# Key and receptance weights: the low halves written by an adding transfer instead of a subtraction on VectorE

## Chip, cores and metric

One core of a Trainium2 chip runs the kernel; the seven others are idle. The metric is the device time of one execution in microseconds (us), taken several times; for the profiled execution there is also a trace, with a span from the first to the last instruction.

## What is computed

The reference is a decoder trunk of two layers over 512 tokens with 1024 channels, in float32: a layer with RWKV-7 time mixing and one with causal differential attention, each between two half-step SwiGLU blocks. The change concerns the time mixing alone, cut here to what matters:

```python
dx = h_prev - h
r, k, v = einsum('sbtc,scd->sbtd', h[None] + dx[None] * mu[:3, None, None, :], w_rkv)   # three 1024x1024 products
...
kk = normalised(k * k_k);  k = k * (1 + (a - 1) * k_a)
y = wkv7_scan(r, decay, k, v, -kk, kk * a)     # S_t = S diag(w) + (S a) b^T + v k^T ; y = S r, 16 heads of 64
...
return (y * g) @ w_o
```

The scan is not done token by token. It is cut into 8 chunks of 64 tokens, and inside a chunk the recurrence becomes small matrix products and the inverse of a triangular matrix per head and chunk.

## The kernel before

**Products in three passes.** TensorE gets a float32 product as three passes over numbers in a reduced format (fp32r): `mm3` (L214 to L217) multiplies high weight by high input, high weight by low input, low weight by high input. So every weight block is kept as two tiles: `whi`, the weight rounded to the reduced format, and `wlo`, what is left of it.

**How a weight block gets there.** `wblock` (L144) has SP load 256 columns of a weight (1 MB) from HBM into a `wraw` buffer (two of them). `halves` (L153) makes, for each of the two 128-column blocks, `whi` with a copy on ACT (L161) and `wlo` with a subtraction on DVE (L162). There are three `whi` and three `wlo` buffers; a block's buffers come free when PE has done its 24 matmuls.

**The time mixing, in order** (`rwkv`). The value product comes first, then the key product (the call of `proj` after `xk = mixed(1)`; eight blocks, here k0 to k7), then receptance (after `xr = mixed(0)`; r0 to r7). In each, one pair of blocks is done row by row, its two blocks taking turns (`by_rows`: k6 with k7, r0 with r1). When a key block is done, `key_done` works on it (`key_cb`) and on the scores of the block two before it (`scores`), which end in DRAM as `md_d`, `am_d` and `boxes`. When a receptance block p is done, `r_done` multiplies it into `Rb` on DVE (L884; the tile is `sR`, called "p's multiply" below).

**The inverses.** `invert` (L829) inverts 128 triangular 32x32 matrices at once on DVE in 31 steps of a multiply (L841) and an add (L842), then copies the transposed result (L844) and stores it into `boxes` with 8 DMAs issued by POOL (L849). It runs twice: `inv0` for heads 0 to 7 (temporary tile `nr_t`), `inv1` for heads 8 to 15 (temporary `nr_a`). Its steps are handed out between the other work (`run`).

**The units.** `wkv` does 16 units (chunk, half of the heads), in stages. Unit 0 begins with a matmul (L971) on `bx`, which SP loads from `boxes` (L946), so after inv0. Units on the second half of the heads come from the fifth unit on. `norm` (L1042 to L1049) has POOL multiply BK with `sR` (L1044, waits for the multiplies of p = 0 to 3 or 4 to 7).

**What sets the order.** A scheduler puts each engine's instructions in a row when the kernel is built; at run time each engine goes through its row and waits by semaphores. DMAs are issued by an engine's queue in that same row: SP's go through a hardware queue (q1), POOL's through a software queue (q0). Before the change the boxes DMAs are the only ones on q0.

```python
self.nc.scalar.copy(hi[:, ks], raw[:, :, c : c + P])                                  # L161, ACT
(eng or self.nc.vector).tensor_sub(lo[:, ks], raw[:, :, c : c + P], hi[:, ks].bitcast(F32))   # L162, DVE
```

Of the kernel before, what the change touches and what calls it, by code (L numbers as in the profile page):

```python
# [10 lines left out]
F32 = mybir.dt.float32  # L11
F32R = mybir.dt.float32r
AF = mybir.ActivationFunctionType
ALU = mybir.AluOpType
PSUM = bass.MemoryType.PSUM

P = 128
T = 512
C = 1024
# [6 lines left out]
class Net:  # L26
# [116 lines left out]
    def wblock(self, src, kt, cols, eng=None, raws=None):  # L143


        raws = raws or [self.tl(self.wp, "wraw", (P, 8, 256), bufs=2)[:, :kt]]
        n = kt // len(raws)
        src = src.rearrange("(k p) f -> p k f", p=P)
        for i, raw in enumerate(raws):
            self.nc.sync.dma_start(raw[:, :, :cols], src[:, i * n : i * n + n, :])  # L150
        return self.halves(raws, kt, cols, eng)

    def halves(self, raws, kt, cols, eng=None):  # L153
        n = kt // len(raws)
        out = []
        for c in range(0, cols, P):
            hi = self.tl(self.wp, "whi", (P, 8, P), F32R, bufs=3)
            lo = self.tl(self.wp, "wlo", (P, 8, P), F32R, bufs=3)
            for i, raw in enumerate(raws):
                ks = slice(i * n, i * n + n)  # L160
                self.nc.scalar.copy(hi[:, ks], raw[:, :, c : c + P])  # L161
                (eng or self.nc.vector).tensor_sub(lo[:, ks], raw[:, :, c : c + P], hi[:, ks].bitcast(F32))  # L162
            out.append((hi, lo))
        return out

# [397 lines left out]
    def rwkv(self, xs, prm):  # L563
# [6 lines left out]
        with ExitStack() as outer:  # L570
# [17 lines left out]
            kt = pa.enter_context(tc.tile_pool(name="kt", bufs=1))  # L588
# [23 lines left out]
            def halves(src):  # L612
                m = src.shape[0]
                hi = self.tl(self.gp, "xgh", dt=F32R, bufs=XB)[:m]
                lo = self.tl(self.gp, "xgl", dt=F32R, bufs=XB)[:m]
                nc.scalar.copy(hi, src)
                nc.vector.tensor_sub(lo, src, hi.bitcast(F32))
                return hi, lo
# [7 lines left out]
            raw = self.tl(self.wp, "wraw", (P, 8, 256), bufs=2)  # L626
# [7 lines left out]
            z = shifted(*pwa, P)  # L634
            nc.scalar.activation(z[0:64], z[0:64], AF.Tanh)
            zh, zl = halves(z)
            pgr = self.ps()
            for k in range(KT):
                self.mm3(pgr[0:64], lr[:, 0, k, :], lr[:, 1, k, :], xg[k][0], xg[k][1], k == 0, k == KT - 1)
            z = shifted(*pg0, P)  # L640
            nc.scalar.activation(z, z, AF.Sigmoid)
            gh, gl = halves(z)
            for k in range(KT):
                nc.sync.dma_start(d["x"][k], xs[k])
# [15 lines left out]
            def mixed(s, eng=None):  # L660

                out = []
                for k in range(KT):
                    i = s * KT + k
                    t = self.tl(kt, "xmt", bufs=2)
                    if s == 2:
                        nc.vector.tensor_scalar_mul(t, h[k][:, 1:], self.omu[:, i : i + 1])
                    else:
                        nc.scalar.activation(t, h[k][:, 1:], AF.Copy, scale=self.omu[:, i : i + 1])
                    nc.vector.scalar_tensor_tensor(t, h[k][:, 0:T], self.v("mu", i), t, ALU.mult, ALU.add)  # L670
                    out.append(self.split(self.gp, t, "xg", XB, eng))
                return out
# [6 lines left out]
            raw = self.tl(self.wp, "wraw", (P, 8, 256), bufs=2).rearrange("p k f -> p (k f)")[:96, :C]  # L679
# [7 lines left out]
            for p in range(KT + 3):  # L687
                if p < KT:
                    c = slice(p * P, (p + 1) * P)
# [7 lines left out]
                if p >= 3:  # L697
                    q = p - 3
                    c = slice(q * P, (q + 1) * P)
# [166 lines left out]
                    run(inv0, 1 if p == 5 else 8)  # L866

            xk = mixed(1)
            last = self.proj(prm["w_rkv"][1], xk, key_done, flush=False, by_rows=C - 256)
            xr = mixed(0)  # L870

            def feed(k):
# [11 lines left out]
                nc.vector.tensor_mul(Rb[:, p, :, 1:], Rb[:, p, :, 1:], ch(ps))  # L884
                run(inv1, 5)

            self.proj(prm["w_rkv"][0], xr, r_done, by_rows=0, feed=feed)
            pa.close()
            run(inv1, 40)
            zs, wb0 = self.wkv(A, BK, Rb, X, fac, d, prm["w_o"])  # L890
# [527 lines left out]
```

## Time and profile before

| | us |
|---|---|
| runs | 2167.19, 2161.10, 2167.46; median 2167.19 |
| profiled execution, device time | 2161.41 |
| its span | 2159.7 (1.7 lie outside) |
| busy in the span: PE | 2108.7 (98%) |
| DVE | 1196.4 (55%) |
| ACT | 821.9 (38%) |
| POOL | 221.4 (10%) |
| granted TensorE clock, mean | 0.991 of full |

PE is busy nearly all the time, so a change can only move the time where PE stands still or is slowed; the shares of the other engines are means over stages that differ. The stage of this change lies between about 440 and 640 us of the span: the key product up to 528, scores up to 537, receptance from 537 to 586, and then the units.

### The profile page before, as it was taken

The numbers are of one execution on the slowest core, as the hardware profiler recorded it, in microseconds if no ns is written. First come the engines' busy times: TensorE is split into PE (matmuls) and PEld (weight loads), VectorE is DVE, ScalarE is ACT, GpSimd is POOL, SyncE is SP. The second block draws the span as 40 slices with busy tenths as digits, with TensorE's granted clock in tenths as the row PEclk, the third lists the DMA queues.
The fourth block names the chain that finished last, engine by engine and source line by source line (L and its number), as shares of the span: only waits on it lengthen the run. The fifth ranks groups of instructions, "written<-read, shape, count | busy, mean of one in ns | idle before, by whom it ended". The sixth has DMA issues, their size and how long they took to land.

```text
span 2159.7 us, 26494 instructions
## 1 busy us (share of the span) xinstructions
PE 2108.7 (98%) x10479; PEld 1770.8 (82%) x10479; DVE 1196.4 (55%) x1876; ACT 821.9 (38%) x1395; POOL 221.4 (10%) x259
## 2 busy tenths in 40 slices
PE   9999999999879999999999999999999999999999
PEld 7888888777779888888888988888889778888887
DVE  6445555798947765444445535445346855444443
ACT  5222324588225444322224443223235854322222
POOL 1101000000332301100000001001010210100000
PEclk9999999999979999999999999999999999999999
DMA  7732333335587632222223223222322112323332
GB/s 251 237 98 88 117 103 103 121 123 136 120 201 187 179 124 89 95 95 96 97 93 103 93 87 98 96 97 97 97 92 85 40 50 91 97 96 97 98 98 78
DMA packets 268760, 239.83 MB, mean 111 GB/s; under 512 B 56922, under 2 KB 253692, under 8 KB 268636
## 3 DMA queue, kind: packets, MB, share of 16 engines
q1 hardware_dynamic: 267868, 236.05, 35.0%
q0 software_dynamic: 768, 2.10, 0.7%
q8 instruction: 82, 1.34, 0.3%
q14 instruction: 42, 0.34, 0.0%
HBM read 202.98 MB, written 28.84 MB: 107 GB/s over the span
## 4 chain that ended last, share of the span: by engine, by line
PE 87%; DVE 6%; ACT 3%; DMA 3%; issue 1%; POOL 1%; SPq 0%; DVEq 0%; ACTq 0%
PE ps L215 27%; PE ps L216 26%; PE ps L217 26%; ACT s L1209 1%; PE ps L1013 1%; DMA boxes<-x 1%; PE ps L977 0%; PE ps L989 0%; PE ps L1012 0%; PE ps L999 0%; POOL boxes L849 0%; DVE x L842 0%; PE ps L1003 0%; PE ps L971 0%; DMA wraw<-in_rwkv_w_rkv_dram 0%
## 5 line engine op out<-in xcount | busy, mean ns | idle before, releaser
L215 PE MATMUL ps<-xgh,whi 128*128 128x512 f32 x1688 | 658.5, 394 | 1.6 <-ACT whi L161 1.0
L216 PE MATMUL ps<-xgl,whi 128*128 128x512 f32 x1688 | 656.0, 390 | 0.0
L217 PE MATMUL ps<-xgh,wlo 128*128 128x512 f32 x1688 | 648.4, 390 | 0.0
L161 ACT CAST whi<-wraw 128x1024 fp32r<-128x1024 f32 (+2 forms) x296 | 303.4, 1029 | 874.2 <-PE ps L216 578.1
L162 DVE TENSOR_TENSOR wlo<-wraw,whi 128x1024 fp32r<-128x1024 f32 (+2 forms) x296 | 427.2, 1447 | 92.4 <-ACT whi L161 83.2
L215 PEld LDWEIGHTS ps<-xgh,whi 128*128 128x128 f32 x1688 | 316.5, 188 | 74.2 <-ACT whi L161 2.7
L216 PEld LDWEIGHTS ps<-xgl,whi 128*128 128x128 f32 x1688 | 317.0, 188 | 66.7 <-issue 1.7
L217 PEld LDWEIGHTS ps<-xgh,wlo 128*128 128x128 f32 x1688 | 316.8, 188 | 65.9
L414 POOL TENSOR_TENSOR u<-u,g 128x512 f32<-128x512 f32 x88 | 124.7, 1417 | 1370.2 <-ACT whi L161 996.3
L216 PE MATMUL ps<-actl,whi 128*128 128x512 f32 x656 | 255.2, 389 | 0.0
L215 PE MATMUL ps<-acth,whi 128*128 128x512 f32 x656 | 254.7, 389 | 0.0
L217 PE MATMUL ps<-acth,wlo 128*128 128x512 f32 x656 | 254.7, 389 | 0.0
L413 DVE TENSOR_TENSOR u<-ps,R 128x512 f32<-128x512 f32 x88 | 60.8, 691 | 287.3 <-PE ps L217 287.3
L456 DVE SCALAR_TENSOR_TENSOR x<-ps,x 128x512 f32<-128x512 f32 x88 | 60.5, 691 | 212.0 <-PE ps L217 212.0
L217 PEld LDWEIGHTS ps<-acth,wlo 128*128 128x128 f32 x656 | 123.1, 188 | 25.7
L215 PEld LDWEIGHTS ps<-acth,whi 128*128 128x128 f32 x656 | 123.1, 188 | 25.6
L216 PEld LDWEIGHTS ps<-actl,whi 128*128 128x128 f32 x656 | 123.1, 188 | 25.4
L215 PE MATMUL ps<-whi,xgh 128*128 128x256 f32 (+1 forms) x384 | 122.8, 323 | 0.2 <-DVE mx L1204 0.2
L216 PE MATMUL ps<-wlo,xgh 128*128 128x256 f32 (+1 forms) x384 | 122.4, 319 | 0.0
L217 PE MATMUL ps<-whi,xgl 128*128 128x256 f32 (+1 forms) x384 | 122.2, 318 | 0.0
L410 DVE TENSOR_TENSOR g<-ps,R 128x512 f32<-128x512 f32 x88 | 60.8, 691 | 109.8 <-PE ps L217 109.7
L222 ACT CAST acth<-u 128x512 fp32r<-128x512 f32 x88 | 54.9, 624 | 124.3 <-POOL u L414 124.2
(332 smaller groups left out, 2262.7 us busy)
## 6 DMA issues: line engine op xcount, KB each, us to landing
wraw<-in_ffn_w_in_dram SPq DMA_DIRECT2D x87, 1024.0 KB, 5.1
wraw<-in_ffn_w_out_dram SPq DMA_DIRECT2D x34, 1024.0 KB, 5.1
boxes<-nr_a SPq DMA_DIRECT2D x64, 192.0 KB, 3.5
wraw<-in_rwkv_w_rkv_dram SPq DMA_DIRECT2D x12, 1024.0 KB, 5.8
wraw<-in_ffn_w_out_dram SPq DMA_DIRECT2D x12, 768.0 KB, 4.4
wraw<-in_w_kv_dram SPq DMA_DIRECT2D x8, 1024.0 KB, 5.4
am_d<-nsq SPq DMA_DIRECT2D x16, 256.0 KB, 2.4
AM<-am_d SPq DMA_DIRECT2D x16, 256.0 KB, 4.4
```

The costliest lines, as they stand in the source:

```text
L161: self.nc.scalar.copy(hi[:, ks], raw[:, :, c : c + P])
L162: (eng or self.nc.vector).tensor_sub(lo[:, ks], raw[:, :, c : c + P], hi[:, ks].bitcast(F32))
L215: mm(ps, wh, xh, start=start, stop=False)
L216: mm(ps, wh, xl, start=False, stop=False)
L217: mm(ps, wl, xh, start=False, stop=stop)
L222: self.nc.scalar.copy(hi, src)
L410: nc.vector.tensor_mul(g, pg, self.R)
L413: nc.vector.tensor_mul(u, pu, self.R)
L414: nc.gpsimd.tensor_mul(u, u, g)
L456: nc.vector.scalar_tensor_tensor(x, ps, 0.5, x, ALU.mult, ALU.add)
L1013: mm(py[:, p, cols], V[:, p, :], KM[:, p, cols], start=c == 0, stop=True)
L1209: nc.scalar.activation(sc, sc, AF.Exp, scale=-1.0, bias=mx[h][:, i, m : m + 1], accum_out=sm[:, h, i, m : m + 1])
```

## The change

For the key and receptance weights, and for no others, `halves` gets `eng = "add"`. ACT writes `whi` as before, and then a second time the same block with its sign turned, rounded to the same format: the negative high half, into `wlo`. Then POOL issues a DMA that reads the block's 128 columns from HBM once more and adds it to what stands in `wlo` (128 x 8 x 128 numbers, 512 KB, in pieces of 512 bytes). That makes 16 subtractions on DVE fewer, 16 activations on ACT more, and 16 DMAs on POOL's queue more. In the changed kernel all lines from L153 on stand 5 lines lower in the time mixing (boxes DMAs L854, `norm` L1049 and L1054, multiplies L889, inverse L846 to L849), the turned copy is L164 and the adding DMA L165.

```diff
@@ wblock @@
-        return self.halves(raws, kt, cols, eng)
+        return self.halves(raws, kt, cols, eng, src)
@@ halves @@
                 self.nc.scalar.copy(hi[:, ks], raw[:, :, c : c + P])
-                (eng or self.nc.vector).tensor_sub(lo[:, ks], raw[:, :, c : c + P], hi[:, ks].bitcast(F32))
+                if eng == "add":
+                    self.nc.scalar.activation(lo[:, ks], raw[:, :, c : c + P], AF.Copy, scale=-1.0)
+                    self.nc.gpsimd.dma_start(lo[:, ks], src[:, i * n : i * n + n, c : c + P], accum_op=ALU.add)
+                else:
+                    (eng or self.nc.vector).tensor_sub(lo[:, ks], raw[:, :, c : c + P], hi[:, ks].bitcast(F32))
@@ rwkv @@
-            last = self.proj(prm["w_rkv"][1], xk, key_done, flush=False, by_rows=C - 256)
+            last = self.proj(prm["w_rkv"][1], xk, key_done, "add", flush=False, by_rows=C - 256)
...
-            self.proj(prm["w_rkv"][0], xr, r_done, by_rows=0, feed=feed)
+            self.proj(prm["w_rkv"][0], xr, r_done, "add", by_rows=0, feed=feed)
```

The scheduler makes another row of it on the engines. Two places matter.

**POOL, from the receptance product to the inverses.** Before, from the last memset of the units' tiles on (`x_520`, `x_521` are inv0's results, `x_518`, `x_519` inv1's; x4 stands for four DMAs):

```order
L925 MEMSET ST_4731 128x512
L1044 TENSOR_TENSOR wraw_4899<-BK_2906,sR_2637 128x512
L1049 TENSOR_TENSOR wraw_4899<-wraw_4899,vec_544 128x512
L1044 TENSOR_TENSOR wraw_5109<-BK_2906,sR_2637 128x512
L1049 TENSOR_TENSOR wraw_5109<-wraw_5109,vec_544 128x512
L849 DMA boxes_75<-x_521_3134 32x32x32 x4
L849 DMA boxes_75<-x_520_3133 32x32x32 x4
L849 DMA boxes_76<-x_519_3132 32x32x32 x4
L849 DMA boxes_76<-x_518_3131 32x32x32 x4
```

and after (`wlo_4466` is r3's low half, `wlo_4545` r4's, `wlo_4550` r5's, `wlo_4629` r6's, `wlo_4634` r7's):

```order
L930 MEMSET ST_4747 128x512
L165 DMA wlo_4466<-in_rwkv_w_rkv_dram 128x8x128
L165 DMA wlo_4545<-in_rwkv_w_rkv_dram 128x8x128
L165 DMA wlo_4550<-in_rwkv_w_rkv_dram 128x8x128
L1049 TENSOR_TENSOR wraw_4915<-BK_2906,sR_2637 128x512
L165 DMA wlo_4629<-in_rwkv_w_rkv_dram 128x8x128
L1054 TENSOR_TENSOR wraw_4915<-wraw_4915,vec_544 128x512
L854 DMA boxes_75<-x_521_3134 32x32x32 x4
L854 DMA boxes_75<-x_520_3133 32x32x32 x4
L165 DMA wlo_4634<-in_rwkv_w_rkv_dram 128x8x128
L1049 TENSOR_TENSOR wraw_5125<-BK_2906,sR_2637 128x512
L1054 TENSOR_TENSOR wraw_5125<-wraw_5125,vec_544 128x512
```

The other 11 adding DMAs (k0 to k7, r0 to r2) stand ahead of the memsets. r6's stands behind a multiply that needs r3's product, and r7's behind all of inv0's boxes DMAs.

**DVE, around the end of inv0.** After the change the four multiplies of p = 0 to 3 are done when inv0 has seven steps to go (`ps_4471` is r3's product, `ps_4554` r4's; `nr_t` belongs to inv0, `nr_a` to inv1):

```order
L889 TENSOR_TENSOR sR_2637<-sR_2637,ps_4471 128x8x64
L846 TENSOR_TENSOR nr_t_4014<-x_520_3133,x_521_3134 128x135
L847 TENSOR_TENSOR x_521_3134<-x_521_3134,nr_t_4014 128x5x27
L846 TENSOR_TENSOR nr_t_4014<-x_520_3133,x_521_3134 128x112
L847 TENSOR_TENSOR x_521_3134<-x_521_3134,nr_t_4014 128x4x28
L846 TENSOR_TENSOR nr_t_4014<-x_520_3133,x_521_3134 128x87
L847 TENSOR_TENSOR x_521_3134<-x_521_3134,nr_t_4014 128x3x29
L846 TENSOR_TENSOR nr_a_4437<-x_518_3131,x_519_3132 128x31
L846 TENSOR_TENSOR nr_t_4014<-x_520_3133,x_521_3134 128x60
```

Before, inv0's closing copy stood behind the multiplies of p = 0 to 6, the subtractions of r2 to r7 and seventeen steps of inv1. Now it stands behind those of p = 0 to 3 and three steps of inv1, which for the rest come after it.

## Rows read from the trace of the kernel before

**Rows 1.** The page: the span, and the engines' busy times.
```profile
span 2159.7 us, 26494 instructions
PE 2108.7 (98%) x10479; PEld 1770.8 (82%) x10479; DVE 1196.4 (55%) x1876; ACT 821.9 (38%) x1395; POOL 221.4 (10%) x259
```

**Rows 2.** Waits of PE, 440 to 640 us: total, times, longest.
```profile
PE ps L971 <- DMA x<-boxes: 18.6, 1, 18.6
PE ps L773 <- ACT nacc L768: 5.3, 3, 3.5
```

**Rows 3.** Timeline of PE: start, duration, then what ran; idle before in brackets.
```profile
604.89 1.94 PE L971 MATMUL ps<-x,x 128*128 128x64 f32 x8 [18.64 <-DMA x<-boxes]
612.79 1.81 PE L971 MATMUL ps<-whi,wlo 128*128 128x64 f32 x8
623.58 1.00 PE L971 MATMUL ps<-x,x 128*128 128x64 f32 x8
```

**Rows 4.** Chain of waits that ended last, 540 to 660 us: start, length, what.
```profile
589.05 1.39 POOL boxes L849
...
595.10 5.61 DMA boxes<-x
600.85 3.51 DMA x<-boxes
```

**Rows 5.** Timeline of DVE: first and last instruction of inv0.
```profile
530.77 0.21 DVE L841 TENSOR_TENSOR nr_t<-x,x 128x31 f32<-128x31 f32 x1
...
589.00 1.02 DVE L844 COPY x<-x 128x1024 f32<-128x1024 f32 x1
```

**Rows 6.** DVE groups by line, 530.7 to 590: busy, mean ns, idle before.
```profile
L162 DVE TENSOR_TENSOR wlo<-wraw,whi 128x1024 fp32r<-128x1024 f32 x6 | 7.3, 1219 | 0.8 <-ACT whi L161 0.8
L841 DVE TENSOR_TENSOR nr_a<-x,x 128x252 f32<-128x252 f32 (+15 forms) x18 | 7.1, 394 | 2.4 <-DMA x<-md_d 2.4
L842 DVE TENSOR_TENSOR x<-x,nr_a 128x255 f32<-128x255 f32 (+15 forms) x17 | 5.8, 344 | 0.0
L884 DVE TENSOR_TENSOR sR<-sR,ps 128x512 f32<-128x512 f32 x7 | 4.7, 673 | 0.0
```

**Rows 7.** Stretches: window, length, busy of each engine, clock, DMA share, GB/s.
```profile
core 0: us, PE busy (x) PEld busy (x) DVE busy (x) ACT busy (x) POOL busy (x), PEclk, DMA share, GB/s
480.00:513.00 33.00, 33.00 (x173) 27.12 (x172) 25.50 (x41) 26.35 (x44) 0.00 (x0) 0.99 0.47 134
513.00:529.00 16.00, 14.93 (x79) 12.18 (x77) 14.51 (x26) 14.90 (x29) 0.00 (x0) 1.00 0.44 100
529.00:537.00 8.00, 7.24 (x51) 6.05 (x52) 7.22 (x18) 7.83 (x16) 0.00 (x0) 1.00 0.74 225
553.00:586.00 33.00, 33.00 (x147) 27.20 (x145) 29.63 (x76) 5.50 (x6) 8.31 (x4) 1.00 0.54 137
605.00:621.00 16.00, 14.63 (x68) 14.26 (x68) 2.99 (x9) 1.18 (x3) 5.27 (x7) 0.51 0.96 233
```

**Rows 8.** Timeline of ACT in the receptance product: the copies that make high halves.
```profile
553.35 2.00 ACT L161 CAST whi<-wraw 128x1024 fp32r<-128x1024 f32 x2
558.85 1.05 ACT L161 CAST whi<-wraw 128x1024 fp32r<-128x1024 f32 x1 [3.50 <-PE ps L216]
568.09 1.06 ACT L161 CAST whi<-wraw 128x1024 fp32r<-128x1024 f32 x1 [8.18 <-DMA wraw<-in_rwkv_w_rkv_dram]
```

**Rows 9.** Line L849, the boxes DMAs: durations on POOL, and time to landing.
```profile
L849 POOL DMA_DIRECT2D boxes<-x x16: 783/783/1390, 589.0 to 608.2; - x16
...
DMA to landing us min/median/max: 3.4/5.2/7.0
```

**Rows 10.** Timeline of POOL: inv0's eight boxes DMAs.
```profile
589.05 6.83 POOL L849 DMA_DIRECT2D boxes<-x  x8 [7.42 <-DVE x L842]
```

**Rows 11.** DMA queues, 440 to 640 us: packets, MB, share of 16 engines.
```profile
q0 software_dynamic: 768, 2.10, 7.1%
```

**Rows 12.** DMA queues, 900 to 1100 us, a feed-forward block, loads of 1 MB.
```profile
q1 hardware_dynamic: 18720, 18.88, 29.0%
```

More of the change, by code (lines that the diff above doesn't have):

```diff
@@ L150, in wblock, with halves @@
             self.nc.sync.dma_start(raw[:, :, :cols], src[:, i * n : i * n + n, :])
-        return self.halves(raws, kt, cols, eng)
-    def halves(self, raws, kt, cols, eng=None):
+        return self.halves(raws, kt, cols, eng, src)
+    def halves(self, raws, kt, cols, eng=None, src=None):
         n = kt // len(raws)
```

## The prediction

> **What bounds the kernel now.** I read the page first: PE is busy for 2108.7 of 2159.7 us [rows 1], so a gain can come only from the 51 us in which it stands still, or from stretches at a low clock. The waits of PE around the change name the one large piece: 18.6 us before L971, the first matmul of unit 0, for a transfer from `boxes` [rows 2]. The timeline places it: receptance ends at 586.2, and unit 0 starts at 604.89 [rows 3]. The price is a little higher than the wait, for the granted clock is 0.51 between 605 and 621, half of full speed, right behind the idle stretch [rows 7].
>
> The chain tells why the boxes are late: POOL issues inv0's DMAs from 589.05 on, they have landed at 600.85, the load takes 3.5 more [rows 4]. POOL starts then because DVE's last instruction of inv0, the copy, begins at 589.00; its first began at 530.77 [rows 5]. So **DVE's row of work between 530.8 and 590.0 sets the start of unit 0**. The groups by line show what else stood in it: six weight subtractions (7.3 us), inv1's steps (7.1 + 5.8), seven multiplies of 0.67, and waits of 0.8 and 2.4 [rows 6].
>
> **What the change takes away.** Ten subtractions lie before 530 and beside busy matmuls; without them nothing ends earlier, since inv0 starts when the key product has given its scores, which PE sets. Inside the 59.2 us of inv0 go: six subtractions, 7.3; inv1's steps but for three, 12.9 - 1.2 = 11.7; three multiplies, 2.0; the two waits, 3.2 [rows 6]. That leaves 59.2 - 24.2 = 35.0 us. DVE alone would have inv0 ready at about 566.
>
> **What it adds on ACT.** Each turned copy is priced like the copy of the high half, 1.05 us [rows 8]. While the key blocks run, ACT is busy 26.35 of 33.00 us [rows 7], and 3.6 blocks bring 3.8 us: hidden by its idle time. From 513 to 537 it isn't: idle are 1.10 and 0.17 us [rows 7], and three turned copies (r0, r1, r2) bring 3.15. So I charge **2 us**: r0 and r1 end at 555.3, not 553.3 (the copies behind them on ACT start at 553.35 [rows 8]). Later ACT is busy 5.50 of 33 us [rows 7]: nothing.
>
> **What the adding transfer costs.** No row shows one. The issue on POOL I take from the boxes DMAs: 0.8 us [rows 9]. For the time that it takes of all 16 DMA engines, E, the nearest rows are those of the same software queue: 16 boxes DMAs of 128 KB took 7.1% of 200 us [rows 11], 0.89 each, so 512 KB take **3.6 us**. The low end is a plain load: 29.0% of 200 us for 18 MB, 3.2 per MB [rows 12], so 1.6 for 512 KB. The high end counts every element twice, since `wlo` has to be read as well as the weight: 7.2. I take 3.6, the same queue and a like kind of piece. Landing: the shortest of the boxes DMAs, 3.4 us [rows 9], plus three more times 0.89, makes 6.1. From buffer free to low half ready it is then 2 x 1.05 + 0.8 + 6.1 = **9.0 us** (7.0 at the low end, some 13 at the high one), where high half plus subtraction took 2.3.
>
> The Trainium skill (DMA: Bandwidth & Descriptors, Anatomy of one DMA — SWDGE (gpsimd) path) fits a DMA from this queue with 2.0 us plus its bytes at 436 GB/s, 3.2 us for this one, an estimate; by it the sum below would come to about 2143. The runs here show 3.4 at least for a quarter of the bytes [rows 9], so I stay with 6.1.
>
> **Which waits follow on PE.** A receptance block takes 33.0 / 6 = 5.5 us [rows 7]. With three buffers a block has 11 us from the end of the block three before it: 9.0 fits, also in the key product, where blocks are further apart. Two don't have 11 us.
> - *r3*: its buffer comes free together with r4's, when the pair r0, r1 ends at 555.3, and only r2 lies between. Ready at 564.3; PE wants it 0.45 into the block, at 561.3: **3.0 us** of waiting. r3 ends at 569.3. r4, r5 and r6 are ready in time (r6's block of weights has landed by 568.09 as before [rows 8]); r6 would end at 585.8.
> - *r7*: on POOL its DMA stands behind inv0's eight boxes DMAs. Inv0 in turn is held by r3: the fourth multiply (0.7), then fifteen short steps (0.21 for the shortest [rows 5], 0.34 to 0.39 in the mean [rows 6]; I take 0.26, they are the narrow ones), then the copy (1.0): 569.3 + 5.6 = 574.9, 15 us earlier than before. Eight boxes issues take 6.8 [rows 10], its own 0.8, landing 6.1: 588.6. PE wants it at 586.3: **2.3 us**. Receptance ends at 593.6.
>
> Unit 0 needs the boxes: 574.9 + 11.8 (589.05 to 600.85) + 4.0 (to 604.89) = 590.7 [rows 3, 4]. So r7's end decides: unit 0 at 593.6 instead of 604.9, **-11.3 us**.
>
> **The clock.** With no long idle time ahead the stretch at 0.51 should go. At most half of its 14.63 us of matmuls comes back, 7.3; but units wait for each other, and the first units' starts are 7.9 us apart at half clock and 10.8 at mixed [rows 3]. I take **-2**.
>
> **Crowding of the DMA engines.** From 555.3 to 593.6 five adding transfers (18.0), the old traffic (0.54 of 33 us, 17.8 [rows 7]) and inv0's boxes, now inside (7.1), ask for 42.9 us of engine time in some 38.7: **+4.2**. In the key product 0.47 x 9.1 + 3.6 = 7.9 of a block's 9.1 us: nothing.
>
> **The sum.** -11.3 - 2 + 4.2 = -9.1. Against the profiled execution (span 2159.7, time 2161.4): 2152.3, so **2152 us**. That execution lies 5.8 under the median of the runs, as does the run of 2161.1; in another set of runs the median may fall on either level. Inv1 ends later than inv0 by about its remaining 25 steps, some 22 us, and is first needed by the fifth unit; it hides. Its boxes also free the buffers for the output weights, whose place in ACT's row has moved back with them.
>
> **Rivals.**
> - *The queue becomes the bound (slower).* One mechanism: E is so large that q0 delivers low halves more slowly than PE uses them. At 7.2 the crowding in receptance is 36.0 + 24.9 - 38.7 = 22.2, and in the key product 0.47 x 9.1 + 7.2 = 11.5 exceeds 9.1 by 2.4, some 7 times: 16.8. Together 39.0 - 13.3 = +25.7: 2187. It outweighs the gain from E = 5.1 on (12 + 2 against 13.3). For it: the sum is already over full at 3.6. Against it: the queue's row gives 3.6. The Trainium skill (Collectives: The Full Stack, The bandwidth ceiling: the fold count and why AG ≠ RS ≠ AR) says that an add in a transfer reads two sources on one ring, and so gets about half the rate; by that rule E would be 7.2 and the time 2187. No run before shows an add. Chance 0.25.
> - *The wait changes its name (no change).* Unit 0 no longer waits for the boxes, but r7's product waits as long for its low half, since POOL holds that DMA back behind inv0 and the boxes. That needs r7's landing some 11 us later, at 600: inv0 late by 4 (ACT late, or the scores that DVE waits for) and the transfer landing 7 later, behind the boxes in the same queue, whose longest was 7.0 [rows 9]. Receptance would end at 605, with the clock's 2 us at most: 2159 to 2163. Chance 0.22.
> - *Transfers cost the low end (faster still).* With E = 1.6 a low half is ready after 7.0: r3 waits 1.0, r7 0.4, unit 0 starts at 589.7, and nothing is crowded: -15.2 - 2, 2144. Chance 0.08.
>
> **How the numbers follow.** My forecast has 0.45: 2144 to 2160, E between 2.5 and 4.5. About 0.3%, 6.5 us, is what a measurement of this kernel can tell from no change. Of the forecast some 0.06 lies within it. Faster: 0.39 + 0.08 = 0.47. Same: 0.06 + 0.20 of the second rival = 0.26. Slower: 0.25 + 0.02 of the second rival = 0.27. The range goes from 2143, just under the low end of E, to 2186, about E = 7.2; more than that leaves out a tenth on the slow side. The likeliest case alone has 2144 to 2160.
>
> **What would show it.** Right: the 18.6 us before unit 0's first matmul are gone or under 3; inv0's copy begins near 574; waits of PE of 2 to 4 us each for r3's and r7's low halves, named as adding transfers; unit 0 near 594; the clock near 1 behind it; an adding transfer lands in 5 to 8 us. Wrong: waits of PE at low halves of key blocks; landings over 10 us; DMA share near 1 from 480 on; or inv0's copy still past 585, since then DVE's own waits, not its work, held it.

## The result and the profile after

The changed kernel takes 2184.06 us (median of 4 runs, 2182.73 to 2186.41), the kernel before 2164.42 beside it: a ratio of **1.0091, interval 1.0075 to 1.0107**. It is slower by some 20 us, where the forecast, 2152 us, lies 12 under the kernel before. The time lies inside the range, near its end, but on the wrong side of no change.

The page of the changed kernel, with the rows that answer to [rows 1], the software queue and the line of the low-half matmuls:

```profile
span 2181.1 us, 26535 instructions
...
PE 2116.6 (97%) x10479; PEld 1774.8 (81%) x10479; DVE 1186.6 (54%) x1860; ACT 836.4 (38%) x1411; POOL 244.3 (11%) x275
...
q0 software_dynamic: 17408, 10.49, 3.8%
...
L222 PE MATMUL ps<-xgh,wlo 128*128 128x512 f32 x1688 | 652.9, 393 | 22.5 <-DMA wlo<-in_rwkv_w_rkv_dram 22.5
```

PE was busy 8 us longer for the same matmuls and idle for 13.5 us more. A wait that wasn't there is now the largest: 22.5 us for low halves. The waits of PE from 440 to 680 us, beside [rows 2]:

```profile
PE ps L222 <- DMA wlo<-in_rwkv_w_rkv_dram: 22.5, 7, 9.4
PE ps L778 <- ACT nacc L773: 6.1, 3, 3.1
PE ps L813 <- issue: 3.3, 1, 3.3
PE ps L1008 <- DMA kbd<-BK: 2.1, 1, 2.1
```

The 18.6 us before unit 0 are gone, as forecast. The timeline of PE places the waits for low halves; four of the seven:

```profile
463.93 0.50 PE L222 MATMUL ps<-xgh,wlo 128*128 128x512 f32 x1 [1.13 <-DMA wlo<-in_rwkv_w_rkv_dram]
473.08 0.80 PE L222 MATMUL ps<-xgh,wlo 128*128 128x512 f32 x1 [5.22 <-DMA wlo<-in_rwkv_w_rkv_dram]
...
494.15 0.50 PE L222 MATMUL ps<-xgh,wlo 128*128 128x512 f32 x1 [2.28 <-DMA wlo<-in_rwkv_w_rkv_dram]
...
617.35 0.79 PE L222 MATMUL ps<-xgh,wlo 128*128 128x512 f32 x1 [9.40 <-DMA wlo<-in_rwkv_w_rkv_dram]
```

The first three are in the key product (k0, k1, k3), the last is r7. The others, 0.96, 1.60 and 1.89, stand in r3 to r6. Read as a table, from the timelines of PE and DVE of both kernels (us from the start of the span; the end of a matmul is taken as 0.23 us after its start, the distance at which they follow each other at full clock):

| | before | after | later by |
|---|---|---|---|
| last matmul of the key product ends | 527.8 | 542.0 | 14.2 |
| inv0's first step | 530.8 | 546.3 | 15.5 |
| receptance ends | 586.1 | 624.2 | 38.1 |
| inv0's copy | 589.0 | 597.6 | 8.6 |
| unit 0 | 604.9 | 624.2 | 19.3 |
| seventh unit | 662.5 | 678.8 | 16.3 |
| end of the span | 2159.7 | 2181.1 | 21.4 |

Receptance comes out 38 us late. The 18.6 us in which PE used to stand before unit 0 take up half of it; the rest is the loss. The stretches, columns as in [rows 7]:

```profile
460.00:480.00 20.00, 13.65 (x50) 10.51 (x49) 9.85 (x17) 10.55 (x17) 2.85 (x2) 0.83 0.91 181
480.00:513.00 33.00, 25.83 (x105) 19.93 (x103) 16.66 (x27) 25.67 (x39) 6.17 (x4) 0.90 0.79 143
...
553.00:586.00 33.00, 32.03 (x170) 27.76 (x169) 23.48 (x58) 15.99 (x28) 7.65 (x11) 0.95 0.99 181
586.00:605.00 19.00, 15.52 (x60) 12.06 (x59) 16.50 (x41) 3.77 (x4) 11.48 (x13) 0.91 1.07 212
605.00:621.00 16.00, 6.59 (x22) 4.95 (x22) 15.14 (x33) 0.00 (x0) 3.82 (x3) 0.69 0.85 154
```

From 480 to 513 the DMA share is 0.79, where it was 0.47, and from 553 on it is about 1 (a packet counts where it starts, so a stretch can come out above 1). The clock (the number ahead of the DMA share) falls in each stretch with a long wait: behind k1's 5.2 us the granted clock was 0.50 from 473.1 to 477.5 us and 1.00 from 477.9 on, so that a wait costs more than its length. DVE is less busy up to 586, as the change meant.

The adding transfers themselves, from the view of their line:

```profile
L165 POOL DMA_DIRECT2D wlo<-in_rwkv_w_rkv_dram x16: 1541/1550/1749, 454.9 to 604.6; - x16
...
DMA to landing us min/median/max: 6.4/9.1/13.3
```

The issue takes 1.55 us on POOL and the landing 9.1 in the median, against 0.8 and 6.1 in the forecast. The longest belongs to k1: issued at 459.74, landed at 473.04.

DVE and POOL at the end of inv0:

```profile
589.26 0.68 DVE L889 TENSOR_TENSOR sR<-sR,ps 128x512 f32<-128x512 f32 x1
...
597.61 1.12 DVE L849 COPY x<-x 128x1024 f32<-128x1024 f32 x1
```
```profile
597.98 6.62 POOL L854 DMA_DIRECT2D boxes<-x  x8 [4.22 <-DVE nr_a L846]
604.58 1.63 POOL L165 DMA_DIRECT2D wlo<-in_rwkv_w_rkv_dram  x1
```

The chain reads: r3's product, its multiply (589.26), inv0's copy (597.61), eight boxes DMAs, and only then r7's transfer at 604.58. It lands 12.7 us later, at 617.3, which ends PE's wait of 9.4.

### The profile page after: what moved, and what is told of

It is laid out like the page before. It is cut to its first block, busy times and chain, and to the rows that moved or that the text cites. A ratio compares the mean times of both kernels' runs of the same rounds, so it can differ in the third digit from the quotient of the medians.

```text
span 2181.1 us, 26535 instructions
## 1 busy us (share of the span) xinstructions
PE 2116.6 (97%) x10479; PEld 1774.8 (81%) x10479; DVE 1186.6 (54%) x1860; ACT 836.4 (38%) x1411; POOL 244.3 (11%) x275
## 4 chain that ended last, share of the span: by engine, by line
PE 85%; DVE 5%; DMA 4%; ACT 2%; issue 2%; SPq 1%; POOL 0%; DVEq 0%; POOLq 0%; ACTq 0%
PE ps L220 26%; PE ps L222 26%; PE ps L221 26%; DMA wlo<-in_rwkv_w_rkv_dram 2%; ACT s L1214 1%; PE ps L1018 1%; PE ps L982 0%; PE ps L994 0%; PE ps L1008 0%; PE ps L976 0%; DVE s L1224 0%; DMA x<-md_d 0%; PE ps L1009 0%; PE ps L1017 0%; PE ps L1004 0%
## 5 line engine op out<-in xcount | busy, mean ns | idle before, releaser
L222 PE MATMUL ps<-xgh,wlo 128*128 128x512 f32 x1688 | 652.9, 393 | 22.5 <-DMA wlo<-in_rwkv_w_rkv_dram 22.5
L167 DVE TENSOR_TENSOR wlo<-wraw,whi 128x1024 fp32r<-128x1024 f32 (+2 forms) x280 | 406.7, 1456 | 96.3 <-ACT whi L162 88.6
```

What stands on the lines that cost most here:

```text
L222: mm(ps, wl, xh, start=False, stop=stop)
```

## The experiments

All kernels are compared with the kernel before, measured beside them on the same chip. Positions are those of the one profiled execution of each.

### One product alone

`key_only` takes `"add"` out of receptance's call, `rec_only` out of the key's:

```diff
-            self.proj(prm["w_rkv"][0], xr, r_done, "add", by_rows=0, feed=feed)
+            self.proj(prm["w_rkv"][0], xr, r_done, by_rows=0, feed=feed)
```

> The adding transfer for the key weights alone; receptance is subtracted on VectorE as before. In the changed kernel the key product ended 14 us later and the receptance product began 19 to 20 us later than before. If the key product's transfers crowd the DMA engines by themselves: waits of PE for low halves of key blocks of 6 to 10 us, the key product's end 12 to 15 us late, inv0's copy and unit 0 late by as much or up to 20, and 13 to 20 us slower in all. If instead the two products only hurt together (the rival): under 5 us slower.

Measured: 2178.37 us, 1.0071 (1.0056 to 1.0086), 15 us. PE waited 8.3 us for low halves of key blocks, the key product ended at 542.5, and unit 0 again waited 19.0 us for the boxes and began at 621.0, 16 late. The first reading holds: the key product loses by itself, and behind it everything moves.

> The adding transfer for the receptance weights alone. Key as before. If the loss is additive: waits of PE for r3 to r7 of 10 to 15 us, receptance's end some 15 to 19 us later, the 18.6 us wait before unit 0 gone, so within 5 us of the kernel before. If the late key product was what spoiled the receptance product: the -9 us of the prediction.

Measured: 2173.80 us, 1.0043 (1.0029 to 1.0057), 10 us: more than the 5 allowed, and nothing of a gain. PE waited 14.8 us for low halves, 6.65 for r3 and 7.43 for r7; receptance ended at 610.2 and unit 0 began there. So my forecast falls for receptance alone, with the key product out of the way. The sum of the two, 25, is somewhat over the 20 of both together.

### Without the transfers, and without the add

```diff
                     self.nc.scalar.activation(lo[:, ks], raw[:, :, c : c + P], AF.Copy, scale=-1.0)
-                    self.nc.gpsimd.dma_start(lo[:, ks], src[:, i * n : i * n + n, c : c + P], accum_op=ALU.add)
```

> The changed kernel without its 16 adding transfers: the low halves of key and receptance stay the negative high halves, so the correction by the low halves is left out. ACT's turned copies and the row of DVE without subtractions stay. If ACT is no bound and the gain was rightly placed: inv0's copy near 570, unit 0 within 3 us of the end of receptance near 590, 14 to 20 us faster than before. If ACT's 16 us or the new order are what costs: no faster than before.

Measured: 2162.44 us, 0.9998 (0.9988 to 1.0008): **no change**: the second reading, and not the gain of 14 to 20 us. Inv0's copy came at 582.2, 7 us earlier and not 19; receptance ended at 591.8, 5.7 later than before; unit 0 began 6.3 earlier, at 598.6, and the seventh unit at 661.8, as before. Its waits of PE, 440 to 680:

```profile
PE ps L975 <- DMA whi<-boxes: 6.6, 1, 6.6
PE ps L777 <- ACT nacc L772: 5.7, 3, 3.1
PE ps L812 <- ACT x L804: 4.5, 1, 4.5
PE ps L993 <- DMA AM<-am_d: 3.0, 1, 3.0
```

The third row is new against [rows 2]: the first scores' matmuls wait for a copy of ACT. That was the first sign that ACT's turned copies aren't hidden.

The other kernel leaves the transfers in and takes the add out (`, accum_op=ALU.add` removed).

> The same 16 transfers of the same pieces from the same queue, but they overwrite the low half and don't add to it, so the low halves hold the weights themselves. If the add costs a second read: the queue's time per transfer falls from 4.0 us of 16 engines to about 2, landing from 9.1 to 5 to 6, and most of the 20 us of loss go. If the pieces of 512 bytes or the queue set the price: 3.5 to 4 us each, and a time within 5 us of the changed kernel.

Measured: 2164.72 us, 1.0001 (0.9992 to 1.0010). Sixteen transfers of the same bytes, pieces and queue cost nothing in the end. PE waited for low halves here too, 9.3 us, 7.9 of them for r7; but receptance ended at 605.8, when before unit 0 began at 604.9: it just used up the slack. **The add is worth the whole loss.** In the traces the rows of all five engines are the same, instruction by instruction, as in the changed kernel, so that nothing but the add differs. The software queue (whole span), and issue and landing of the plain transfers:

```profile
q0 software_dynamic: 17408, 10.49, 3.3%
...
L165 POOL DMA_DIRECT2D wlo<-in_rwkv_w_rkv_dram x16: 873/873/1073, 454.7 to 588.5; - x16
...
DMA to landing us min/median/max: 4.7/6.7/9.5
```

### The price of one transfer

Two blocks only, k4 and r5, by transfer; the rest is subtracted as before. `two_copies` leaves the add out. (A letter for each block says which way it goes.)

```diff
-                if eng == "add":
+                if (eng[c // P] if isinstance(eng, str) else eng) == "a":
...
-            last = self.proj(prm["w_rkv"][1], xk, key_done, "add", flush=False, by_rows=C - 256)
+            last = self.proj(prm["w_rkv"][1], xk, key_done, "ssssasss", flush=False, by_rows=C - 256)
...
-            self.proj(prm["w_rkv"][0], xr, r_done, "add", by_rows=0, feed=feed)
+            self.proj(prm["w_rkv"][0], xr, r_done, "sssssass", by_rows=0, feed=feed)
```

> The kernel before with only two blocks, k4 and r5, by adding transfer, so that no other adding transfer runs near them. It measures the price of one. If the median landing of 9.1 us in the changed kernel comes from the transfers crowding each other: landing 6 to 6.5 us here, 4 us of 16 engines each or less. If one add costs that much by itself: landing 8 to 9 us. PE waits for neither block in both cases (11 us from the buffer's release to its use).

> The same two transfers without the add, so that the low halves of k4 and r5 hold the weights themselves. If the add itself is the surcharge: landing 2 to 3 us under that of the two adding transfers, and the issue on POOL 0.87 us where the adds take 1.55. If not: the same landing.

For k4, in a quiet place, the queue from 470 to 495 us and the landing, first with the add, then without:

```profile
q0 software_dynamic: 1040, 0.52, 16.9%
...
DMA to landing us min/median/max: 6.7/6.7/6.7
```
```profile
q0 software_dynamic: 1040, 0.52, 11.0%
...
DMA to landing us min/median/max: 4.7/4.7/4.7
```

Alone, the adding transfer takes 16.9% of 25 us, 4.2 us of all 16 engines, and lands after 6.7; the plain one takes 2.75 and lands after 4.7. The add costs half as much again, and 2 us. In company the two come nearer: with the boxes' 14.2 us taken off, the queue's 3.8% and 3.3% of the span make 4.3 us for an adding transfer and 3.6 for a plain one. r5, amid the loads for the units, landed after 10.7 and 10.5: there, in this one place, the company set the time, with or without the add. So both readings hold in part: of the 9.1 us, 6.7 are the transfer's own, and 2.4 come with company. PE waited about 1 us for one of the two blocks in either kernel, where I had expected none. The two kernels have one time each (2162.94 and 2166.09 us), which says nothing about a difference in time.

### Is unit 0's wait worth its length?

`inv0_first` is the kernel before, with inv1's steps issued behind inv0's copy:

```diff
+                    self.copy0 = self.inv_copy.ins
...
-                run(inv1, 5)
+                with tc.issue_after(self.copy0):
+                    run(inv1, 5)
```

> The kernel before, all subtractions on VectorE, with one thing changed: inv1's steps are issued only after inv0's copy, so no step of inv1 stands in front of it. If the 18.6 us wait before unit 0 is really worth its length: inv0's copy 4 to 10 us earlier, unit 0 as much earlier, and the time falls by 4 to 10 us. If what unit 0 gains is given back in the units that follow (as in the run without transfers, where unit 0 came 6.3 us earlier and the seventh unit at the same time as before): unit 0 earlier, the time within 3 us of before.

Measured: 2160.89 us, 0.9994 (0.9982 to 1.0005). Inv0's copy came 7.3 us earlier, unit 0 6.0, the last unit 4.2 (750.6 for 754.8), and no change in time can be told. A small gain isn't excluded, the full length is. Inv1's copy had moved from 602.1 to 614.6.

`pool_sub_inv0` adds to it that POOL does receptance's subtractions (`nc.gpsimd` in the place of `"add"`).

> A candidate: the kernel before with inv0 first as in the first run of this set, and receptance's eight subtractions on POOL, no transfers and no turned copies. A subtraction of this size should take POOL some 2.5 us (1.26 for half of it in the trace of before). If VectorE's row of work sets unit 0 and unit 0 sets the time: inv0's copy near 575, unit 0 within 4 us of receptance's end at 586 to 590, 10 to 18 us faster than before. If the following units give it back: within 4 us of before.

Measured: 2168.55 us, 1.0023 (1.0012 to 1.0034): slower. POOL took 2.52 us each, as assumed, and unit 0 began at 600.2, earlier than before. But inv1's boxes were issued at 622.5, where they were at 602.4, and the fifth unit waits for them:

```profile
644.89 1.97 PE L974 MATMUL ps<-x,x 128*128 128x64 f32 x8 [8.21 <-DMA x<-boxes]
```

It began at 644.9, where it began at 644.4 before: the whole lead of unit 0 was gone. The loss comes behind it, where the granted clock was 0.79 to 656 us and 0.86 to 668 (1.00 for these two units before) and PE waited 2.4 us for `kbd`; the seventh unit began at 668.4, 5.8 late. A second chain lies close behind the first: what inv0 gains by going first, inv1 loses.

### r7 alone back on VectorE

The changed kernel with `"aaaaaaas"` for receptance.

> The changed kernel with one block, r7, subtracted on VectorE again; the other 15 by adding transfers. In the changed kernel PE waited 9.4 us for r7's low half, whose transfer was issued behind inv0's boxes. If that place in POOL's row costs what PE waits there: the wait goes, receptance ends 8 to 12 us earlier and the time falls by 5 to 12 us against the changed kernel. If unit 0 then waits for the boxes instead: the time falls by under 4 us.

Measured: 2187.74 us, 1.0108 (1.0089 to 1.0127): no better than the change. r7's wait is gone and receptance ends at 613.1, 11 us earlier. But PE then waits before unit 0, and the fifth unit waits for inv1's boxes:

```profile
618.60 1.94 PE L976 MATMUL ps<-x,x 128*128 128x64 f32 x8 [5.40 <-issue]
...
662.24 1.97 PE L976 MATMUL ps<-x,x 128*128 128x64 f32 x8 [7.60 <-DMA x<-boxes]
```

For the first wait the profile names no cause ("issue"); the last of inv0's boxes had landed at 614.6, 4.0 us earlier, and before the change unit 0 followed them by 4.2, so the boxes are the likely cause, not a shown one. Inv1's boxes were issued at 640.6, 8 us later than in the changed kernel. So r7's 9.4 us are the last link of a chain that had been late long before, and not a cost that can be taken off by itself.

### ACT's turned copies

`extra_act` adds them to the kernel before; the subtraction then overwrites what they wrote.

```diff
                     self.nc.scalar.activation(lo[:, ks], raw[:, :, c : c + P], AF.Copy, scale=-1.0)
-                    self.nc.gpsimd.dma_start(lo[:, ks], src[:, i * n : i * n + n, c : c + P], accum_op=ALU.add)
+                    self.nc.vector.tensor_sub(lo[:, ks], raw[:, :, c : c + P], hi[:, ks].bitcast(F32))
```

> The kernel before with ACT's 16 turned copies added and nothing taken away: each low half is first written by ACT and then overwritten by VectorE's subtraction; no transfer. If ACT's copies are what put off the end of receptance by 5.7 us in the run without transfers: receptance ends 4 to 7 us later than before, waits of PE for the squares of the key blocks grow, and the time is 3 to 8 us over before. If they hide: within 2 us of before.

Measured: 2176.18 us, 1.0057 (1.0037 to 1.0077), 12 us: more than expected. The first scores waited 4.6 us for ACT, as without transfers, and receptance ended at 596.9, 10.8 late. Part of it may be this kernel's own, since each subtraction now waits for a copy more; no run parts it.

`neg_pool_nt` has no transfers either, and the turned copies on POOL:

```diff
-                    self.nc.scalar.activation(lo[:, ks], raw[:, :, c : c + P], AF.Copy, scale=-1.0)
+                    self.nc.gpsimd.tensor_scalar_mul(lo[:, ks], raw[:, :, c : c + P], -1.0)
```

> The changed kernel without its transfers, and with the turned copies on POOL and not on ACT; the low halves of key and receptance stay the negative high halves, so the correction by the low halves is left out. If ACT's copies ate the gain of the freed VectorE (about 12 us each): the key product and the scores end as before, receptance near 586, 6 to 13 us faster than before. If the freed VectorE is worth nothing: within 3 us of before.

Measured: 2157.95 us, **0.9971 (0.9961 to 0.9980)**, 6.3 us faster than before. The wait of the scores for ACT is gone, and from 480 to 513 PE is busy throughout; that stretch without and with ACT's copies (`neg_pool_nt`, then `no_transfer`):

```profile
480.00:513.00 33.00, 33.00 (x176) 27.27 (x175) 22.52 (x36) 26.07 (x44) 11.85 (x4) 1.00 0.43 116
```
```profile
480.00:513.00 33.00, 28.48 (x137) 23.55 (x136) 18.67 (x32) 25.79 (x41) 0.00 (x0) 0.90 0.39 108
```

So the freed VectorE is worth some 6 us, and ACT's copies cost the same 6 (from 0.9971 to 0.9998). Unit 0 began at 596.5, 8.4 earlier than before. Here inv1 came earlier as well (its copy at 596.7, before 602.1), and most of the lead lasted: the last unit began 6.5 us earlier.

> The changed kernel with the turned copies on POOL and not on ACT, transfers as in the change. If the loss is ACT's copies and the landing of the transfers, one beside the other: 6 to 12 us faster than the changed kernel, some 8 to 14 us slower than before, with PE's waits for low halves as long as in the changed kernel. If the transfers are late only because ACT is: waits for low halves under 8 us in all, and within 4 us of before. If POOL's copy is slow (over 3 us each): as slow as the changed kernel, with longer waits for low halves.

Measured: 2182.12 us, 1.0090 (1.0066 to 1.0113), as slow as the change. By its time this is the third reading, but only in part by its mechanism: POOL's copy took 3.0 us in the mean, and the waits for low halves came to 20.1, not more than the 22.5 of the changed kernel. The key product ended at 528.4, 0.6 later than before, with 4.2 us of such waits in it. But it had begun 2.4 us earlier: it took 68.4 us, where `neg_pool_nt` took 62.5 and the kernel before 65.4. So the adding transfers lengthen the key product by 6.0 us without ACT's copies, and by 11.0 beside them (68.9 in `no_transfer`, 79.8 in the changed kernel). Receptance lost the rest: it ended at 619.3, with 13.3 us of waiting for r7.

### Only the blocks with slack

`rec_456` has `"ssssssss"` for key and `"ssssaaas"` for receptance; `inv0_456` has inv0 first as well.

> Adding transfers for r4, r5 and r6 alone: the blocks that have 11 us from buffer to use, no transfer behind the boxes DMAs on POOL, no turned copy where ACT is busy. Key product as before. If the loss comes from the blocks without slack, from ACT in the key product and from crowding: no wait of PE for a low half over 1 us, receptance's end within 2 us of before, inv0's copy 2 to 6 us earlier, the time within 4 us of before. If an adding transfer costs wherever it stands: 3 to 6 us slower.

Measured: 2162.08 us beside 2166.62, **0.9984 (0.9975 to 0.9994)**: faster than both kernels, by little, some 3.5 us. The median of the kernel before itself differs by 3.2 us from one set of runs to another (2163.4 to 2166.6), so this gain, though clear beside its own set, is a small one. The waits weren't as expected; PE, 440 to 690 us:

```profile
PE ps L976 <- DMA x<-boxes: 11.3, 1, 11.3
PE ps L222 <- DMA wlo<-in_rwkv_w_rkv_dram: 6.1, 2, 4.3
```

The two waits are r4's and r6's. Receptance ended 6 us late. But these 6 us lie inside the wait before unit 0, which shrank to 11.3, and unit 0 began 1.2 us earlier than before, the seventh unit 3.9.

> A candidate: r4, r5 and r6 by adding transfers, and inv1's steps issued only after inv0's copy. VectorE then has three subtractions and all of inv1 fewer before the copy: copy near 575 to 578, unit 0 near 592 to 595, 10 to 13 us earlier than before. If half of it lasts, as with inv0 first alone (unit 0 6.0 us earlier, the last unit 4.2): 4 to 7 us faster than before. If inv1, later by 10 to 15 us, holds up the fifth unit: no faster.

Measured: 2161.86 us, 0.9982 (0.9971 to 0.9993). Unit 0 began at 596.0, 8.9 earlier, but from the sixth unit on (649.8 and 650.2) the two kernels run level: inv1's copy was at 612.6, and nothing of the further gain lasts.

## Why the prediction was wrong

By its own steps:

- **"What bounds the kernel now"** named the right wait and the wrong price. Unit 0 did wait for inv0 on DVE, and the wait went. But "unit 0 earlier by 11.3" was taken as time, and no run gave that: 6.0 us earlier with inv0 first gave nothing that can be told from no change, 8.4 gave 6.3 at best, where inv1 came earlier too. I put inv1 at nothing, since it was "first needed by the fifth unit; it hides". It hid by little: inv0's lead came out of inv1, and the fifth unit waited for it in `pool_sub_inv0` (8.2 us) and `r7_sub` (7.6).
- **"What the change takes away": 35 us of DVE's row.** Inv0 took 51.3 us (546.33 to 597.61), and 48.7 without any transfer. I had added up work and taken DVE to be its limit. With less to do it waited for others: of the 51.4 us from 546.3 to 597.7 it was busy for 39.4 and idle for 12.0. Its largest waits there, and two steps near the end of inv0:

```profile
DVE nsq L817 <- DMA am_d<-nsq: 5.5, 1, 5.5
DVE nr_a L816 <- DMA boxes<-nr_a: 3.4, 1, 3.4
DVE nr_a L846 <- DMA x<-md_d: 1.6, 1, 1.6
```
```profile
590.19 1.14 DVE L847 TENSOR_TENSOR x<-x,nr_t 128x135 f32<-128x135 f32 x1
591.37 2.53 DVE L846 TENSOR_TENSOR nr_t<-x,x 128x112 f32<-128x112 f32 x1
```

Steps of these sizes take some 0.3 us elsewhere; while these two ran, POOL did the two multiplies of `norm` and issued r6's transfer. (Before the change, too, two steps beside such multiplies took 1.2 us each.) From the multiply of r3's product to the copy it took 8.4 us, where I had 4.6.

- **"What it adds on ACT": 2 us.** The runs without transfers give 5.8 (0.9971 to 0.9998), with other rows from the scheduler in each. I had compared busy time with idle time over 33 us [rows 7] and called it hidden. What counts is the row: a copy of 1.05 us ahead of the scores' copies delayed them, PE waited 4.5 us, and the clock fell behind the wait.
- **"What the adding transfer costs": E = 3.6, landing 6.1, issue 0.8.** Measured for one in a quiet place: 4.2, 6.7 and 1.58 to 1.75; in the kernel 9.1 and up to 13.3 to landing. The landing counts from the start of the issue, so that my sum had the issue in it twice: it should have read 2.1 + 6.1 = 8.2 us from buffer to low half. Measured are 2.1 + 9.1 = 11.2 in the median and 15.4 at the longest, before any delay in ACT's row. This is the step that failed most: **"with three buffers a block has 11 us ... 9.0 fits, also in the key product"**. It didn't: k0, k1 and k3 cost PE 8.6 us, and the key product ended 14 us late. Its first blocks aren't 9.1 us apart: before the change k0 and k1 follow the value product back to back (48 matmuls from 462.35 to 473.9). The add made the difference, since plain transfers of the same bytes landed after 6.7 and cost nothing.
- **"Crowding": nothing in the key product.** (In receptance the window is 593.6 - 555.3 = 38.3 us and not 38.7, so that the sum gives +4.6.) The mean over a block hid what comes together. From 455 to 475 us three adding transfers and the ordinary traffic asked for 1.1 of the engines:

```profile
q0 software_dynamic: 3065, 1.55, 62.0%
q1 hardware_dynamic: 2624, 3.15, 48.4%
```

With plain transfers it was 0.99 in the same window, at no loss, so a full window isn't by itself what costs.

- **"Which waits follow": r3 3.0 and r7 2.3.** Both waits came, in another size: 0.96 for r3 (6.65 in `rec_only`) and 9.4 for r7 (13.3 in `neg_pool`). Those of k0, k1, k3 and of two blocks between r3 and r7 (1.60, 1.89) weren't foreseen. The ring is closed: r3's product holds inv0, inv0's boxes hold r7's transfer, r7 holds the end of receptance. Each late transfer goes round it.
- **"The clock": -2.** The slow stretch behind unit 0's start went (1.00 from 624 to 640 us, before 0.51 from 605 to 621), but others came with each new long wait (0.83, 0.90, 0.69 in the rows above).

Of what I had named as signs of being wrong, three came in full: waits at low halves of key blocks, landings over 10 us, and inv0's copy past 585. The DMA share rose to 0.79 from 480 us and was near 1 from 553. That the time still lies inside the range is due to its slow end, which stands on the first rival.

Of the rivals, the first came true by its sign and nearly by its number (2187 for 2184), but not by its mechanism. It wanted 7.2 us of engine time for a transfer and a queue that can't keep up; measured are 4.2 to 4.3, and the loss comes from late landings in places without slack. ACT's copies make it worse in the key product, but aren't needed for it: `neg_pool`, without them, is as slow. The Trainium skill (Collectives: The Full Stack, The bandwidth ceiling: the fold count and why AG ≠ RS ≠ AR) says of the reduce step of a ring that the second source read halves the rate; that it holds for an adding load was my own step. By the quiet pair of runs the add takes 1.5 times the engine time of a plain transfer (4.2 for 2.75), and in company 1.2 times (4.3 for 3.6), less than its 2. The rule pointed the right way in that the add is not free, and I gave it 0.25 when my own row for a price had no add in it.

What the runs add up to, by the ratios and in this order: VectorE freed -6.3 us, ACT's copies +5.8, transfers as such +0.7 (the intervals overlap), the add +19.5. Only the last step is pure; in the others the scheduler made other rows too. And the steps don't stand alone: with the copies on POOL, adding transfers take the time from 0.9971 to 1.0090, some 26 us, and `extra_act` puts ACT's copies at 12. How the add's number splits between the landing and the longer issue on POOL is open for most blocks. For k1, with the longest wait of the key product, it was the landing: issued at 459.46 and 459.74, it landed 7.8 us later without the add and 13.3 with it, of which the longer issue can explain 0.7. More low-half buffers, which would tell, were not tried.

## What to carry to other kernels

When work is moved from an engine to a transfer, price its landing in company and not alone, and set it against the time that each single block has between buffer and use: here 11 us for most blocks and 6 for r3, and 11.2 were needed in the median, 15.4 at the longest. Take only the blocks whose delay falls into a wait that is there anyway: three of sixteen still cost PE 6.1 us, but ahead of unit 0, and gave a small gain where all sixteen lost 20 us. And before a wait's length is booked as gain, look for the next chain that ends near it: only the distance to that one can be gained.

## What the runs showed of the hardware

An adding transfer of 512 KB held POOL for 1.55 us at its issue, a plain one of the same shape for 0.87, with the same count of packets (1040); boxes DMAs of 128 KB took 0.78 [rows 9]. Alone it took 4.2 us of the 16 engines where the plain one took 2.75. And a wait of PE of 5.2 us was followed by 4.4 us at a granted clock of 0.50, in which matmuls came 0.43 us apart and not 0.23. That is 2 us more, so that the stall of one transfer cost about 1.4 times what the view of the waits shows for it.
